# Scores, transposes and weighted sums of all attention heads two weight tiles later in a two-layer encoder trunk

## The chip, the cores and the metric

The kernel runs on one core of one Trainium2 chip. The time is device microseconds of one execution; the kernel before takes 844.85 us, the median of 3 runs (843.68 to 844.89). A core has five engines that work side by side: PE (matrix products), DVE, ACT and POOL (elementwise work) and SP, which here only issues transfers. Each works through its own instructions in the order in which they stand, and waits where one needs what another engine or a transfer has not delivered yet.

## The reference

A trunk of two layers on 256 frames of 1024 features. Each layer normalizes x, projects it with w_in, and gives the columns to four mixers: A, attention in chunks with a table of position biases; B, latent attention with a rotary key; C, attention with a forgetting gate; D, a causal convolution of 31 taps. Each of A, B and C has 4 heads of 64. Their outputs are projected, gated, summed and projected again; an MLP with squared ReLU follows.

```python
def hybrid_layer(x, positions, ...):
    h = rms_norm(x, g_mix)
    a_q, a_k, a_v, b_qlat, b_kvlat, b_krope, c_q, c_k, c_v, c_f, d_val, d_gate = split(h @ w_in)
    out_a = chunk_band_attention(a_q, a_k, a_v, rel_bias)          # 4 heads
    q = rms_norm(b_qlat, g_q_lat) @ w_uq                           # and rotary embedding of a part
    kv = rms_norm(b_kvlat, g_kv_lat) @ w_ukv
    out_b = block_causal_attention(q, k, v, CHUNK)                 # 4 heads; k: kv's and the rotary key
    log_f = log_sigmoid(c_f + b_forget)
    out_c = block_causal_attention(c_q, c_k, c_v, 1, cumsum(log_f))   # 4 heads
    out_d = silu(layer_norm(causal_conv(d_val * sigmoid(d_gate), w_dw) + b_dw))
    proj = einsum('bsnc,ncd->bsnd', [out_a, out_b, out_c, out_d], w_branch)
    gates = sigmoid(h @ w_gate + b_gate)
    x = x + sum(gates * proj, axis=2) @ w_o
    hf = rms_norm(x, g_ffn)
    return x + square(relu(hf @ w_up)) @ w_down
```

## The kernel before

**Weights.** All weights stream through the core once, as tiles of 128x1024 float32 (512 KB; a few are smaller). `weights` (line 102 on) makes one tile ready: SP issues its transfer into `raw` (line 110; five buffers), ACT rounds it to `hi` (line 114), and `lo` = raw − hi is made at line 115 on DVE, or, while `share[1]` is 2, on POOL for every second tile. Each product is then three matmuls that add up (`mm3`, lines 122 to 124): high by high, high by low and low by high. A tile of w_in, of the values or of the gates keeps PE busy for some 2.8 us.

**Stages of a layer.** `qk(0)` and `qk(2)` take two w_in tiles each (queries and keys of mixer A; then the convolution's input), `values` four tiles (v0 to v3 here; product pv), `mla` the tiles uq and ukv of mixer B, `qk(4)` and `qk(6)` two tiles each; then 32 tiles of gates, two per call of `gates(g)`, 8 tiles of the branches (`branch(m)`, product pbr), 8 of w_o (product po, into the four PSUM banks that held the halves of the last two branches' pbr, each free when line 737 has read it), and the MLP (w_up, w_dn).

**Small work between the tiles.** After each weight tile the code calls `tick()`, which runs the next entry of a list, `side`. Attention is spread over it: head i has its scores at entry A0 + 2i, its transposes three entries later and its weighted sum four entries later. Heads 0 to 3 are mixer A's, 4 to 7 B's, 8 to 11 C's. The other entries have fixed numbers: the latents of mixer B at 0 with their transposes at 1 to 3 (plt; their low half is latl, line 294), the rotary key's transposes (pkr, line 449) at 4, the rotary tables at 5, the forgetting sums at 13, the convolution's taps (cacc, lines 488 and 491) at 4 to 24, its normalization at 25 to 29.

```python
        NT = A0 + 2 * NH + 3
        plan = [[] for _ in range(NT)]
        for i in range(NH):
            plan[A0 + 2 * i].append((2, scores, i))
            plan[A0 + 2 * i + 3].append((1, transposes, i))
            plan[A0 + 2 * i + 4].append((0, weighted, i))
        ...
        for g in range(16):
            gates(g)
            if side:
                continue
            share[1] = 0
            if nbr < 0:
                conv_silu(last_exp[0])
            else:
                branch(nbr)
```

Entry 0 is run after qk(0)'s first tile, entry 4 after v0, entry 6 after v2, entry 8 after mla, entries 13 + 2g and 14 + 2g after the two tiles of `gates(g)`. When the list is empty, share[1] goes to 0, and each later call of `gates` is followed by one piece: first `conv_silu`, then one branch each. The branches that are left come one behind the other after the last gates.

**What `scores` does** (line 555 on): two matmuls into S from the queries and keys (qkA for mixer A; DVE writes it at lines 634 and 636); for a head of mixer A, SP issues the transfer of its bias table `bt` (192 KB, line 558, two buffers), and POOL writes two memsets into it (line 560) as soon as it is there. DVE and ACT follow with the softmax.

**What `branch` does**: eight products for each of two halves a into pbr; DVE multiplies each half by the gates Z (line 737, yt); POOL adds the parts (lines 738 and 739); ACT rounds the sum to yh (line 740); DVE makes the low half yl (line 741).

**What sets the order.** PE's instructions stand in the order of the code. Those of the other engines are put in order by a scheduler when the kernel is built, by its own estimate, so the diff alone doesn't tell it.

Of the kernel before, what the change touches and what calls it, by code (L numbers as in the profile page):

```python
# [44 lines left out]
NSMALL = 123  # L45


A0 = 4
CONV_FROM, CONV_TO = 4, 25
WARM = 9  # L50

# [19 lines left out]
def hybrid_trunk(ctx: ExitStack, tc: tile.TileContext, xT, xtok, pos, small, gfin, abias, w_lat, w_v, w_in, w_uq, w_ukv,  # L71
# [253 lines left out]
    for l in range(L):  # L325
# [349 lines left out]
        NH = 3 * HEADS  # L675
# [6 lines that stand above are left out]
        side = [[(lambda f=f, i=i: f(i)) for _, f, i in sorted(p, key=lambda e: e[0])] for p in plan]  # L682
# [285 lines left out]
```

## Time and profile before

| | us |
|---|---|
| median of 3 runs | 844.85 (843.68 to 844.89) |
| profiled execution | 845.43 |
| its span | 843.6 |
| outside the span | 1.8 |
| PE busy | 826.0 (98%) |
| DVE busy | 569.9 (68%) |
| ACT busy | 450.0 (53%) |
| POOL busy | 152.7 (18%) |

The span is the time from the first to the last instruction that the profiler recorded. The names L110, L115 and so on are lines of the kernel's code. PE at 98% means that all stretches in which PE stood still sum up to some 18 us, of which a part lies at the very start and the very end. The matmul records overlap (a matmul's start is 0.23 us or 0.12 us behind the one before it, while its own duration is longer), so on PE one reads the starts. "Idle before" in brackets is the time for which an engine had nothing to do ahead of an instruction, with the instruction whose end released it.

### The profile page before, as it was taken

Reading aid. Unit: us, or ns where it says so; the run is one execution under the profiler, and the core shown is the slowest. Engines: PE = TensorE matmul, PEld = TensorE weight load, DVE = VectorE, ACT = ScalarE, POOL = GpSimd, SP = SyncE. Lnnn points to the kernel's source line nnn. Section 1 sums busy time; section 2 is a strip of 40 time slices with the busy share of each in tenths; the row PEclk is TensorE's granted clock in tenths of the full one; section 3 lists DMA queues with packets and bytes.
Section 4 is the critical chain, followed back from the end, with each engine's and each line's share of the span. In section 5 each row is a group of like instructions: output and inputs, shape, how many; then the busy total and the mean of one; then the engine's idle time right before and its main releaser. Section 6 shows DMA issues by size and latency. Waiting matters only on the chain.

```text
span 843.6 us, 14520 instructions
## 1 busy us (share of the span) xinstructions
PE 826.0 (98%) x5646; PEld 759.5 (90%) x5646; DVE 569.9 (68%) x950; ACT 450.0 (53%) x759; POOL 152.7 (18%) x156
## 2 busy tenths in 40 slices
PE   9989999999999999999999999999999999999996
PEld 8969999999889999999899899999998899999994
DVE  7889984787665555555578899557866655555554
ACT  6745646654464444544485764485445554545443
POOL 6524332124200000000004332312331000000000
PEclk9999999999999999999999999999999999999999
DMA  8655433555546555555554544345555555555531
GB/s 281 232 181 181 132 126 126 166 184 185 165 164 198 189 189 186 186 189 187 172 176 161 188 132 145 132 131 174 194 176 200 175 186 190 191 185 186 188 126 50
DMA packets 42549, 145.55 MB, mean 173 GB/s; under 512 B 5104, under 2 KB 7408, under 8 KB 42352
## 3 DMA queue, kind: packets, MB, share of 16 engines
q1 hardware_dynamic: 41904, 142.98, 52.1%
q10 hardware_dynamic: 576, 1.64, 0.5%
q8 instruction: 44, 0.72, 0.4%
q14 instruction: 25, 0.20, 0.1%
HBM read 143.55 MB, written 1.05 MB: 171 GB/s over the span
## 4 chain that ended last, share of the span: by engine, by line
PE 89%; DVE 5%; issue 2%; POOL 1%; ACT 1%; DMA 0%; SPq 0%; POOLq 0%; DVEq 0%; ACTq 0%
PE pgt L122 7%; PE pgt L123 7%; PE pgt L124 7%; PE pu L123 7%; PE pu L124 7%; PE pu L122 7%; PE pd L123 7%; PE pd L122 7%; PE pd L124 7%; PE S L555 2%; DVE lo L115 2%; PE pqk L122 2%; PE pPV L593 2%; PE pqk L123 2%; PE pqk L124 2%
## 5 line engine op out<-in xcount | busy, mean ns | idle before, releaser
L115 DVE TENSOR_TENSOR lo<-raw,hi 128x1024 fp32r<-128x1024 f32 (+3 forms) x241 | 300.5, 1250 | 195.9 <-ACT hi L114 193.9
L114 ACT CAST hi<-raw 128x1024 fp32r<-128x1024 f32 (+2 forms) x273 | 278.5, 1024 | 266.0 <-issue 208.0
L122 PE MATMUL pgt<-xgh,hi 128*128 128x256 f32 x512 | 149.5, 292 | 0.0
L122 PE MATMUL pu<-xgh,hi 128*128 128x256 f32 x512 | 144.9, 283 | 0.7 <-ACT xgh L293 0.7
L123 PE MATMUL pu<-xgl,hi 128*128 128x256 f32 x512 | 145.1, 283 | 0.3
L124 PE MATMUL pu<-xgh,lo 128*128 128x256 f32 x512 | 144.9, 283 | 0.0
L123 PE MATMUL pgt<-xgl,hi 128*128 128x256 f32 x512 | 144.7, 283 | 0.0
L124 PE MATMUL pgt<-xgh,lo 128*128 128x256 f32 x512 | 144.7, 283 | 0.0
L122 PE MATMUL pd<-hi,u 128*128 128x512 f32 x256 | 100.8, 394 | 1.6 <-ACT u L803 1.6
L123 PE MATMUL pd<-hi,u 128*128 128x512 f32 x256 | 100.7, 393 | 1.1 <-DVE u L804 1.1
L122 PEld LDWEIGHTS pu<-xgh,hi 128*128 128x128 f32 x512 | 98.0, 191 | 3.4 <-ACT xgh L293 1.1
L123 PEld LDWEIGHTS pu<-xgl,hi 128*128 128x128 f32 x512 | 98.0, 191 | 3.0 <-DVE xgl L294 0.7
L124 PE MATMUL pd<-lo,u 128*128 128x512 f32 x256 | 99.6, 389 | 0.0
L122 PEld LDWEIGHTS pgt<-xgh,hi 128*128 128x128 f32 x512 | 97.9, 191 | 0.8 <-issue 0.3
L123 PEld LDWEIGHTS pgt<-xgl,hi 128*128 128x128 f32 x512 | 98.1, 192 | 0.4
L124 PEld LDWEIGHTS pu<-xgh,lo 128*128 128x128 f32 x512 | 98.0, 191 | 0.0
L124 PEld LDWEIGHTS pgt<-xgh,lo 128*128 128x128 f32 x512 | 97.9, 191 | 0.0
L115 POOL TENSOR_TENSOR lo<-raw,hi 128x1024 fp32r<-128x1024 f32 (+1 forms) x32 | 77.4, 2419 | 111.2 <-ACT hi L114 106.5
L491 DVE SCALAR_TENSOR_TENSOR cacc<-up,sm,cacc 128x256 f32<-128x256 f32 x120 | 77.9, 693 | 0.0
L122 PEld LDWEIGHTS pd<-hi,u 128*128 128x128 f32 x256 | 48.3, 189 | 10.8 <-ACT u L803 2.4
L124 PEld LDWEIGHTS pd<-lo,u 128*128 128x128 f32 x256 | 48.1, 188 | 10.4
L123 PEld LDWEIGHTS pd<-hi,u 128*128 128x128 f32 x256 | 48.3, 189 | 9.7 <-DVE u L804 2.0
(255 smaller groups left out, 1358.3 us busy)
## 6 DMA issues: line engine op xcount, KB each, us to landing
raw<-in_w_gate SPq DMA_DIRECT2D x64, 512.0 KB, 3.7
raw<-in_w_up SPq DMA_DIRECT2D x64, 512.0 KB, 4.2
raw<-in_w_dn SPq DMA_DIRECT2D x64, 512.0 KB, 4.2
raw<-in_w_in SPq DMA_DIRECT2D x23, 512.0 KB, 4.2
raw<-in_w_br SPq DMA_DIRECT2D x16, 512.0 KB, 3.7
raw<-in_w_o SPq DMA_DIRECT2D x16, 512.0 KB, 4.3
raw<-in_w_v SPq DMA_DIRECT2D x8, 512.0 KB, 4.2
raw<-in_w_lat SPq DMA_DIRECT2D x8, 210.0 KB, 4.6
```

Of the source, the lines that this page charges most:

```text
L114: cut = nc.scalar.copy(hi[:, c:c + w], raw[:, c:c + w])
L115: done = eng.tensor_tensor(lo[:, c:c + w], raw[:, c:c + w], hi[:, c:c + w], op=ALU.subtract)
L122: nc.tensor.matmul(ps, sh, mh, start=first, stop=False)
L123: nc.tensor.matmul(ps, *((sl, mh) if late_mov else (sh, ml)), start=False, stop=False)
L124: nc.tensor.matmul(ps, *((sh, ml) if late_mov else (sl, mh)), start=False, stop=last)
L491: ins = nc.vector.scalar_tensor_tensor(cacc[:, c, :], up[:, c, j:j + T], wcol, cacc[:, c, :], op0=ALU.mult, op1=ALU.add)
L555: nc.tensor.matmul(sl, q[:, b * P:(b + 1) * P], k[:, 0:n], start=True, stop=True)
L593: nc.tensor.matmul(po[o:o + 64, 0:T], v[:, 0, vo:vo + HD], pts[:, 0:T], start=True, stop=False)
```

## The change

One number: the entry of the list at which the first head's scores stand goes from 4 to 6.

```diff
--- before.py
+++ after.py
@@ -45,7 +45,7 @@
 NSMALL = 123
 
 
-A0 = 4
+A0 = 6
 CONV_FROM, CONV_TO = 4, 25
 WARM = 9
 
```

Scores, transposes and weighted sums of every head move two entries back, in both layers. The list has 33 entries instead of 31, so it is empty after g = 9 instead of g = 8: one more lo per layer is made by POOL, and conv_silu and the branches between the gates begin one call of `gates` later, so that three branches instead of two follow the last gates. All fixed entries stay.

On PE, behind the first values tile (v0, pv; numbers behind a name count the kernel's tiles), this stood before:

```order
L122 MATMUL pv_680<-hi_682,xgh_164 128x512
L123 MATMUL pv_680<-hi_682,xgl_165 128x512
L124 MATMUL pv_680<-lo_683,xgh_164 128x512
L555 MATMUL S_699<-qkA_381 128x128 [waits DVE_49]
L555 MATMUL S_699<-qkA_381 128x256
L449 MATMUL pkr_717<-ident,kr_70_585 128x128 [waits PE_49]
L449 MATMUL pkr_717<-ident,kr_70_585 128x128
L122 MATMUL pv_679<-hi_727,xgh_164 128x512 [waits Activation_49]
```

And now:

```order
L122 MATMUL pv_680<-hi_682,xgh_164 128x512
L123 MATMUL pv_680<-hi_682,xgl_165 128x512
L124 MATMUL pv_680<-lo_683,xgh_164 128x512
L449 MATMUL pkr_699<-ident,kr_70_585 128x128 [waits DVE_49]
L449 MATMUL pkr_699<-ident,kr_70_585 128x128
L122 MATMUL pv_679<-hi_709,xgh_164 128x512 [waits Activation_49]
L123 MATMUL pv_679<-hi_709,xgl_165 128x512
L124 MATMUL pv_679<-lo_710,xgh_164 128x512 [waits Pool_49]
```

S of the first head is gone from here (it stands behind the third values tile, v2), and pkr, which stays, is now the first to wait for DVE.

On SP, from the transfer behind v0 on, before (in_w_v are the values tiles v1 to v3, in_abias the tables bt):

```order
L558 DMA bt_702<-in_abias 128x384
L110 DMA raw_726<-in_w_v 128x1024
L110 DMA raw_753<-in_w_v 128x1024
L558 DMA bt_774<-in_abias 128x384
L110 DMA raw_792<-in_w_v 128x1024
L110 DMA raw_821<-in_w_uq 128x1024
```

And now:

```order
L110 DMA raw_708<-in_w_v 128x1024
L110 DMA raw_735<-in_w_v 128x1024
L558 DMA bt_756<-in_abias 128x384
L110 DMA raw_774<-in_w_v 128x1024
L558 DMA bt_860<-in_abias 128x384
L110 DMA raw_797<-in_w_uq 128x1024
```

Both tables moved: the first behind v2, the second behind v3. On POOL the tables' memsets stand where they stood; after the change it reads (lo_644 is the low half of the fourth w_in tile, lo_710 that of v1, lo_776 that of v3; before, the rows are the same but for the tables' numbers, and the values' lo's carry 728 and 794):

```order
L115 TENSOR_TENSOR lo_543<-raw_541,hi_542 128x1024
L231 MEMSET tq 128x2x64 x2
L560 MEMSET bt_756 64x64 x2
L560 MEMSET bt_860 64x64 x2
L115 TENSOR_TENSOR lo_644<-raw_642,hi_643 128x1024
L115 TENSOR_TENSOR lo_710<-raw_708,hi_709 128x1024
L115 TENSOR_TENSOR lo_776<-raw_774,hi_775 128x1024
```

The memsets of both tables stay ahead of lo_644.

On DVE, around the last two branches of layer 0 (yt_2629 is branch 6, yt_2672 branch 7, each with two halves; lo_2749 and lo_2767 are low halves of w_o tiles), before:

```order
L737 TENSOR_TENSOR yt_2629<-pbr_2630,Z_1099 128x512
L737 TENSOR_TENSOR yt_2629<-pbr_2644,Z_1099 128x512
L115 TENSOR_TENSOR lo_2749<-raw_2747,hi_2748 128x1024
L741 TENSOR_TENSOR yl_1992<-yt_2629,yh_1991 128x256
L737 TENSOR_TENSOR yt_2672<-pbr_2673,Z_1099 128x512
L737 TENSOR_TENSOR yt_2672<-pbr_2687,Z_1099 128x512
L115 TENSOR_TENSOR lo_2767<-raw_2765,hi_2766 128x1024
```

And now, where branch 5 (yt_2586) belongs to the group:

```order
L737 TENSOR_TENSOR yt_2586<-pbr_2587,Z_1076 128x512
L737 TENSOR_TENSOR yt_2586<-pbr_2601,Z_1076 128x512
L115 TENSOR_TENSOR lo_2731<-raw_2729,hi_2730 128x1024
L741 TENSOR_TENSOR yl_2054<-yt_2586,yh_2053 128x256
L737 TENSOR_TENSOR yt_2629<-pbr_2630,Z_1076 128x512
L737 TENSOR_TENSOR yt_2629<-pbr_2644,Z_1076 128x512
L115 TENSOR_TENSOR lo_2749<-raw_2747,hi_2748 128x1024
L737 TENSOR_TENSOR yt_2672<-pbr_2673,Z_1076 128x512
L741 TENSOR_TENSOR yl_2054<-yt_2629,yh_2053 128x256
L737 TENSOR_TENSOR yt_2672<-pbr_2687,Z_1076 128x512
```

Branch 5's yt and yl now stand directly ahead of branch 6's, and yl of branch 6 between the two halves of branch 7's yt.

## Rows read from the trace of the kernel before

**Rows 1.** The page: busy time of the engines, and the chain by engine.
```profile
PE 826.0 (98%) x5646; PEld 759.5 (90%) x5646; DVE 569.9 (68%) x950; ACT 450.0 (53%) x759; POOL 152.7 (18%) x156
...
PE 89%; DVE 5%; issue 2%; POOL 1%; ACT 1%; DMA 0%; SPq 0%; POOLq 0%; DVEq 0%; ACTq 0%
```
**Rows 2.** Waits of PE, whole span: us in total, times, longest us.
```profile
PE S L555 <- DVE qkA L636: 3.3, 1, 3.3
...
PE po L122 <- DVE yt L737: 0.6, 2, 0.3
```
**Rows 3.** Timeline of PE, 46.1 to 51.6: start us, us, instruction, idle before.
```profile
46.23 0.39 PE L124 MATMUL pv<-lo,xgh 128*128 128x512 f32 x1
49.91 0.92 PE L555 MATMUL S<-qkA 64*128 64x128 f32 x4 [3.29 <-DVE qkA L636]
```
**Rows 4.** Stretch by engine: us, busy (instructions) PE to POOL, PEclk, DMA, GB/s.
```profile
51.30:54.60 3.30, 3.30 (x9) 2.63 (x8) 3.30 (x11) 3.23 (x8) 0.00 (x0) 0.50 0.56 204
```
**Rows 5.** Timeline of DVE, 38 to 51.
```profile
38.20 3.35 DVE L115 TENSOR_TENSOR lo<-raw,hi 128x1024 fp32r<-128x1024 f32 x1
...
44.20 3.39 DVE L491 SCALAR_TENSOR_TENSOR cacc<-up,sm,cacc 128x256 f32<-128x256 f32 x3
47.52 1.21 DVE L115 TENSOR_TENSOR lo<-raw,hi 128x1024 fp32r<-128x1024 f32 x1
48.65 0.47 DVE L294 SCALAR_TENSOR_TENSOR latl<-plt,sm,lath 128x256 fp32r<-128x256 f32 x1
...
49.44 0.74 DVE L636 TENSOR_TENSOR qkA<-pqk,rb 128x256 f32<-128x256 f32 x2
```
**Rows 6.** Timeline of POOL, 29 to 48.
```profile
37.86 0.23 POOL L560 MEMSET bt<- 64x64 f32 x2 [4.53 <-DMA bt<-in_abias]
38.06 5.75 POOL L115 TENSOR_TENSOR lo<-raw,hi 128x1024 fp32r<-128x1024 f32 x2
```
**Rows 7.** Timeline of SP, 28 to 42: start of each issue.
```profile
28.80 0.33 SPq L110 DMA_DIRECT2D raw<-in_w_v  x1
29.18 0.42 SPq L558 DMA_DIRECT2D bt<-in_abias  x1
...
32.72 0.43 SPq L558 DMA_DIRECT2D bt<-in_abias  x1
35.51 0.33 SPq L110 DMA_DIRECT2D raw<-in_w_v  x1
40.49 0.33 SPq L110 DMA_DIRECT2D raw<-in_w_uq  x1
```
**Rows 8.** DMA issues of Rows 7's first four: KB each, us from issue to landing.
```profile
raw<-in_w_v SPq DMA_DIRECT2D x1, 512.0 KB, 3.8
...
bt<-in_abias SPq DMA_DIRECT2D x1, 192.0 KB, 3.9
...
bt<-in_abias SPq DMA_DIRECT2D x1, 192.0 KB, 5.1
...
raw<-in_w_v SPq DMA_DIRECT2D x1, 512.0 KB, 6.9
```
**Rows 9.** Timeline of PE, 40.3 to 41.1.
```profile
40.87 0.28 PE L124 MATMUL pqk<-xgh,lo 128*128 128x256 f32 x1
```
**Rows 10.** Timeline of DVE, 212 to 223, last branches of layer 0.
```profile
215.06 1.28 DVE L737 TENSOR_TENSOR yt<-pbr,Z 128x512 f32<-128x512 f32 x2
...
219.91 0.43 DVE L741 TENSOR_TENSOR yl<-yt,yh 128x256 fp32r<-128x256 f32 x1 [2.45 <-ACT yh L740]
220.26 1.28 DVE L737 TENSOR_TENSOR yt<-pbr,Z 128x512 f32<-128x512 f32 x2
```
**Rows 11.** Timeline of PE, 217.7 to 222.5, first products of w_o.
```profile
217.86 0.40 PE L122 MATMUL po<-hi,yh 128*128 128x512 f32 x1
...
221.09 0.47 PE L122 MATMUL po<-hi,yh 128*128 128x512 f32 x1 [0.31 <-DVE yt L737]
```
**Rows 12.** Timeline of DVE, 624 to 634, last branches of layer 1.
```profile
630.51 0.43 DVE L741 TENSOR_TENSOR yl<-yt,yh 128x256 fp32r<-128x256 f32 x1 [2.44 <-ACT yh L740]
```

## The prediction

> **What bounds the kernel now.** I read the page first: PE is busy for 826.0 us of the span and the chain of work that ended last is 89% PE, 5% DVE [rows 1]. So nearly every us of the kernel is matmul time, which this change doesn't touch (the number of matmuls stays), and what can move are the stretches in which PE stands still. The list of PE's waits gives them: the largest is one wait of 3.3 us of the first score product S for DVE's qkA of line 636; among the rest are 0.6 us in two places of po for DVE's yt of line 737 [rows 2]. Then I read PE's own timeline at the first of them: the first values tile's last matmul starts at 46.23, S at 49.91, "3.29" idle [rows 3]. So PE is free at 46.62 and gets going at 49.91. Behind it PE's granted clock is 0.50 for 3.3 us, from 51.3 to 54.6 [rows 4], its lower level of 1.2 GHz: work of 3.3 us there would be 1.65 us at full clock, so the wait costs 3.29 + 1.65, about 4.9 us in all. This is the most that taking the wait away could bring.
>
> DVE's timeline says why qkA is late. In order it does a lo (subtraction that makes the low half of a weight tile) in 3.35 us at 38.20, where the same shape takes 1.21 at 47.52; three convolution taps (cacc) in 3.39; the lo of 47.52; and latl at 48.65 [rows 5]. In the same stretch POOL runs two lo's, 38.06 to 43.81 [rows 6]. So DVE is slow there because POOL works beside it.
>
> **The change, part by part.** A0 from 4 to 6 moves scores, transposes and weighted sums of all 12 heads two weight tiles back, in both layers, and whatever hangs on the last of them by one gates pair (two tiles).
>
> (1) The first heads. PE's next instruction behind the first values tile is no longer S but pkr (transpose of the rotary key), which isn't moved. In the order of after, pkr waits for a DVE instruction too: latl, which shares its PSUM pool of two buffers. In the trace of before that latl is the one that starts at 48.65 and takes 0.47 [rows 5], so it ends at 49.12. If nothing else moved, PE would wait from 46.62 to 49.17: 2.55 instead of 3.29, a gain of 0.74 and no more. The wait would change its name, not go.
>
> (2) But S brings its bias table along. Each of the first four heads has SP load bt (192 KB) and POOL write two memsets into it, and both are issued where the scores stand. Before, SP's order is v0, bt0, v1, v2, bt1, v3 (v: values tiles); in the order of after it is v0, v1, v2, bt0, v3, bt1. POOL's order is the same in both at this place: memsets of bt0, memsets of bt1, then the lo of the fourth w_in tile (lo_644). So that lo now stands behind a table which is loaded behind the fourth values tile. Its dates: SP issues v3 at 35.51 [rows 7] and it lands after 6.9 us [rows 8], at 42.4. bt lands some 0.5 us after the tile ahead of it: v0 28.80 + 3.8 = 32.6, bt0 29.18 + 3.9 = 33.1 [rows 7, 8]. As v3 now has one table fewer ahead of it (0.5 us) and bt1 comes behind it, bt1 lands between 42.4 and 42.9; I take 42.75. (Before: 32.72 + 5.1 = 37.8 [rows 7, 8], and POOL's memsets start at 37.86 at once, after an idle 4.53 [rows 6].) From landing to the start of the lo it was 38.06 − 37.82 = 0.24. The first of the two lo's takes 38.06 to 40.49, the moment at which SP issues the uq tile that waits for it [rows 6, 7]: 2.43. So lo_644 is ready at 42.75 + 0.24 + 2.43 = 45.42. PE needs it at the first L124 of that tile, 40.87 [rows 9]; before, it was there 0.4 us ahead. **PE waits 4.55 us** at a place where it didn't wait.
>
> Bounds of this: landing 42.4 and 2.43 for the lo give 4.2; landing 42.9 and 3.3 for the lo (the second of the two lo's, 5.75 − 2.43 [rows 6]) give 5.6. I take 2.43, since what lengthened the second was DVE's lo of 38.20, which is over by then.
>
> The Trainium skill ("SBUF — State Buffer", section "Who interferes with whom") says that a DVE instruction with two SBUF inputs and a GpSimd one that reads SBUF shut each other out for the whole instruction, whichever starts first. The trace agrees: 38.06 + 2.43 = 40.49 is when DVE's blocked lo could start, and with 1.06 more it ends at 41.55, as its row says; POOL's second lo then ran from there to 43.81. By that rule the moved lo would lose at most one tap of DVE, about 0.5 us, and the upper end would be 5.2 instead of 5.6; the sum stays.
>
> What the stall takes over: the first values tile then ends at 46.62 + 4.55 = 51.17. DVE has meanwhile worked on without POOL beside it (its lo of 38.20 in 1.21), and even in before's slow order latl is done at 49.12, qkA of line 636 at 49.44 + 0.74 without the stall. So pkr at 51.17 doesn't wait, and S, two tiles on, doesn't either. Net of (1) and (2): −3.29 + 4.55 = **+1.26 us**.
>
> (3) The clock. Before, a stop of 3.29 us was followed by 3.3 us at 0.50 [rows 3, 4]. A stop of 4.55 will be followed by such a stretch too; I take the same cost, 1.65, and so a difference of 0. From no such stretch to twice the one of before it is −1.65 to +1.65.
>
> (4) Layer 1's start. There the tables of heads 0 and 1 are loaded during layer 0 and PE doesn't wait at S at all (the wait list has it once [rows 2]). Nothing to gain; 0.
>
> (5) The end of attention. The plan is over one gates pair later. Before, 7 of the 8 branch products stand between gates pairs, and branches 6 and 7 back to back at the end; after, 6, so branches 5, 6 and 7 follow each other and then w_o. A branch takes PE 2.86 us, but its sum goes DVE yt (two products of 0.64), POOL two additions, ACT yh, DVE yl, and yl is in DVE's queue ahead of the next branch's yt: yt of branch 6 starts at 215.06, yl at 219.91 after an idle 2.45, yt of branch 7 at 220.26 [rows 10]. So one turn of it takes 5.2 us against PE's 2.86. In before, PE comes out of branch 7 at 217.86, has four PSUM banks to reuse in w_o, and waits for the third, freed by yt of branch 7: due 217.86 + 12 × 0.23 = 220.62, started 221.09 [rows 11], 0.47 late. After, with T the end of branch 5 on PE: yt(5) T + 0.06; yl(5) 4.85 later at T + 4.9; yt(6) T + 5.26 to 6.46; a lo; the first half of yt(7) T + 7.6 to 8.25; yl(6) T + 5.26 + 4.85 = 10.1; the second half of yt(7) T + 10.45 to 11.1, as the order puts it behind yl(6). PE ends branch 7 at T + 5.72. First bank: free with half of yt(6), T + 6.09 in place of 5.72, 0.37. Third bank, T + 8.85: free since 8.25. Fourth, due at T + 10.23: free at 11.3, 1.07. Together 1.44 against 0.47: **+0.97 in each layer** (layer 1 has the same shape, yl at 630.51 after 2.44 idle [rows 12]), +1.94. Bounds: 0.25 a layer, if only the first bank is late by more than before, and 1.5, if the fourth is late by another half turn.
>
> (6) One more lo per layer on POOL, since share[1] stays 2 for one pair longer. POOL is busy for 18% of the span [rows 1] and takes 2.4 us for it instead of DVE's 1.21. Cover: POOL's idle time; where it stands ahead of POOL's small power of the convolution's variance, up to 1 us a layer could show. I take 0.
>
> Sum: +1.26 + 0 + 1.94 = **+3.2 us**. The profiled execution, 845.43 us with a span of 843.6, would become 848.6; it is 0.58 above the median of the runs, so the median of 844.85 becomes **848.0**.
>
> **Rivals.**
> A. *The wait goes as the change says* (faster). bt1 lands early enough for lo_644, and DVE has latl done by 46.6: −3.29 − 1.65 + 1.94 = −3.0, 841.8. For it: the table has only 192 KB, and DVE needs just 2.6 us less work. Against it: SP's order puts the table behind v3, and in before DVE worked without a break up to 49.1 while POOL ran its lo's early.
> B. *The table is in time, latl isn't* (same). Wait of 2.55 at pkr instead of 3.29, clock as before, tails: −0.74 + 1.94 = +1.2, 846.0. It decides if bt1 lands before 38.2, as its 192 KB would if transfers in flight at once shared evenly. For a landing in between, say 40, the lo ends at 42.7, PE waits 1.8, and the sum lies between A and B, near 844, same too.
> C. *The tails don't show* (same): only +1.26, 846.1. It decides if the scheduler's order of yl and yt costs PE nothing, as where POOL and ACT are faster than in [rows 10].
> D. *A second stretch at 0.50* (slower): the stop of 4.55 costs twice 1.65, or POOL's extra lo shows with 1 us: +5 to +6, 850.0.
>
> **How the numbers follow.** The measurement can tell about 0.2%, 1.7 us, from no change: faster is below 843.2, slower above 846.5. Forecast 0.58, A 0.09, B 0.15, C 0.10, D 0.08. Slower: forecast and D, 0.66; same: B and C, 0.25; faster: A, 0.09. The forecast's own bounds are +1.26 −0.35 to +1.05 and tails 0.5 to 3.0: 846.3 to 850. To hold 8 in 10 the range takes in B and C below and most of D: 845.6 to 850.2; A and the lowest of B lie outside.
>
> **What would show it.** Step 2: a wait of PE of 4 to 5 us at L124 of pqk for POOL's lo at about 40.9, POOL's memset idle until 42.4 or later, and no wait at S. If instead the list names pkr with 2.5 us, B holds; if it names neither, A. Step 3: a stretch at 0.50 right behind the stall. Step 5: waits of po for yt of 1 to 1.5 us in each layer in place of 0.6 in all; if these are gone, C. The forecast is wrong as a whole if bt's transfer overtakes the tile ahead of it.

## The result

The changed kernel takes 857.03 us, the median of 4 runs (856.68 to 857.37), against 844.87 for the kernel before: the ratio is 1.0146, with a 95% interval of 1.0129 to 1.0164. It is slower by 12.2 us; the forecast was 3.2 us slower, 848.0 with a range of 845.6 to 850.2. The sign was right, the size was not.

The page of the kernel after, its span and its busy times:

```profile
span 855.1 us, 14522 instructions
...
PE 826.5 (97%) x5646; PEld 759.5 (89%) x5646; DVE 579.3 (68%) x948; ACT 449.2 (53%) x759; POOL 156.2 (18%) x158
```

PE is busy as long as in [rows 1] (826.5 against 826.0), so the 11.5 us by which the span grew from 843.6 are time in which PE stands still. The list of PE's waits, to be held against [rows 2] (us in total, times, longest):

```profile
PE pPV L593 <- ACT pts L584: 6.4, 8, 1.3
PE pqk L124 <- POOL lo L115: 5.6, 1, 5.6
...
PE po L122 <- DVE yt L737: 1.5, 2, 0.8
...
PE plat L122 <- ACT hi L114: 1.0, 2, 0.5
```

The wait of 3.3 us at S is gone. In its place stands the stall at L124 of the fourth w_in tile that the prediction worked out, 5.6 us; the waits of w_o grew by 0.9 us; and eight waits of pPV (the weighted sums of the heads, line 593) for ACT's pts (the copy of the transposed probabilities, line 584), 6.4 us, are new. The prediction has no step for these. The plat waits lie ahead of 20 us, where the two kernels have the same order: PE's first 22 us simply ran 0.4 us later in this execution.

**The stall.** POOL between 29 and 56, SP between 28 and 60, and the two transfers with their us to landing, in the kernel after:

```profile
38.54 0.23 POOL L560 MEMSET bt<- 64x64 f32 x2 [5.54 <-DMA bt<-in_abias]
44.41 0.23 POOL L560 MEMSET bt<- 64x64 f32 x2 [5.64 <-DMA bt<-in_abias]
44.61 4.66 POOL L115 TENSOR_TENSOR lo<-raw,hi 128x1024 fp32r<-128x1024 f32 x2
```

```profile
35.91 0.33 SPq L110 DMA_DIRECT2D raw<-in_w_v  x1
36.28 0.86 SPq L558 DMA_DIRECT2D bt<-in_abias  x1
```

```profile
raw<-in_w_v SPq DMA_DIRECT2D x1, 512.0 KB, 8.0
...
bt<-in_abias SPq DMA_DIRECT2D x1, 192.0 KB, 8.1
```

The second table landed at 36.28 + 8.1 = 44.4, POOL's lo started at 44.61, and PE went on at 46.99:

```profile
46.99 0.58 PE L124 MATMUL pqk<-xgh,lo 128*128 128x256 f32 x1 [5.56 <-POOL lo L115]
```

The clock behind it, from the busy times by stretch (the third number from the right is the granted clock):

```profile
46.30:46.90 0.60, 0.00 (x0) 0.00 (x0) 0.00 (x0) 0.00 (x0) 0.60 (x1) 0.62 0.00 0
46.90:49.80 2.90, 2.81 (x13) 2.81 (x14) 0.00 (x0) 0.00 (x0) 2.37 (x2) 0.50 0.61 204
49.80:53.00 3.20, 3.20 (x21) 2.90 (x21) 1.59 (x5) 1.42 (x2) 0.77 (x1) 0.99 0.95 331
```

PE worked 2.9 us at its lower level, 1.45 us lost, against 1.65 in [rows 4]. This holds for this one execution; in the traces of four experiments with the same stall the stretch at 0.50 is twice as long (last section).

**The waits of pPV.** The first stands at 84.61, "1.22" idle. DVE, then ACT, then POOL and PE of the kernel after, around it:

```profile
75.72 1.21 DVE L115 TENSOR_TENSOR lo<-raw,hi 128x1024 fp32r<-128x1024 f32 x1
76.85 3.40 DVE L491 SCALAR_TENSOR_TENSOR cacc<-up,sm,cacc 128x256 f32<-128x256 f32 x3
80.17 1.72 DVE L634 SCALAR_TENSOR_TENSOR QC<-pqk,rb 64x256 f32<-64x256 f32 x4
81.92 0.29 DVE L570 CUSTOM_DVE_ANT_0 neg<-S,bt 128x128 f32<-128x128 f32 x1
```

```profile
82.26 0.40 ACT L572 ACTIVATE pe<-neg,mn 128x128 f32<-128x128 f32 x1 [5.77 <-DVE mn L570]
...
83.15 1.03 ACT L114 CAST hi<-raw 128x1024 fp32r<-128x1024 f32 x1
84.09 0.47 ACT L584 COPY pts<-pT 128x384 f32<-128x384 f32 x1
```

```profile
76.57 2.61 POOL L115 TENSOR_TENSOR lo<-raw,hi 128x1024 fp32r<-128x1024 f32 x1 [0.92 <-ACT hi L114]
```

```profile
76.20 0.92 PE L555 MATMUL S<-qkA 64*128 64x128 f32 x4
...
84.61 0.65 PE L593 MATMUL pPV<-pts,VAC 128*64 128x256 f32 x2 [1.22 <-ACT pts L584]
```

PE finishes S of a head (the third of mixer A) at about 77.1. DVE's first step of its softmax (neg, line 570) comes only at 81.92, since three convolution taps, 3.40 us beside POOL's lo of 76.57, and four copies stand ahead of it in DVE's queue. ACT's exp (pe) waits for it for 5.77 us; and behind pe, in ACT's queue, stands pts, which belongs to the head before and whose own input has been there since 80.5. PE is through with the tile ahead at 83.4 and waits 1.22 us for pts. So one late DVE instruction holds, through ACT's order, a matmul of another head. In the kernel before, the same entry of the list holds the scores of the fourth head (S at 75.79), and DVE does this there:

```profile
73.77 1.21 DVE L115 TENSOR_TENSOR lo<-raw,hi 128x1024 fp32r<-128x1024 f32 x1
74.91 1.27 DVE L491 SCALAR_TENSOR_TENSOR cacc<-up,sm,cacc 128x256 f32<-128x256 f32 x3
76.10 0.85 DVE L634 SCALAR_TENSOR_TENSOR QC<-pqk,rb 64x256 f32<-64x256 f32 x2
76.98 0.29 DVE L570 CUSTOM_DVE_ANT_0 neg<-S,bt 128x128 f32<-128x128 f32 x1
```

There the taps are through when POOL's lo starts (at 76.16), and neg comes 1.2 us behind the start of S instead of 5.7. The kernel after also puts four of the copies ahead of neg instead of two. Over all 24 heads neg starts 1.0 to 3.4 us behind S in the kernel before, and no pPV waits; in the kernel after seven heads of each layer are 2.2 to 5.7 us behind, and four of each layer's weighted sums wait.

### The profile page after: what moved, and what is told of

It is laid out like the page before. It is cut to its first block, busy times and chain, and to the rows that moved or that the text cites. A ratio compares the mean times of both kernels' runs of the same rounds, so it can differ in the third digit from the quotient of the medians.

```text
span 855.1 us, 14522 instructions
## 1 busy us (share of the span) xinstructions
PE 826.5 (97%) x5646; PEld 759.5 (89%) x5646; DVE 579.3 (68%) x948; ACT 449.2 (53%) x759; POOL 156.2 (18%) x158
## 4 chain that ended last, share of the span: by engine, by line
PE 88%; DVE 3%; ACT 3%; issue 2%; POOL 2%; DMA 1%; SPq 0%; POOLq 0%; DVEq 0%; ACTq 0%
PE pgt L122 7%; PE pu L123 7%; PE pgt L123 7%; PE pu L124 7%; PE pu L122 7%; PE pgt L124 7%; PE pd L123 7%; PE pd L122 7%; PE pd L124 7%; PE S L555 2%; ACT hi L114 2%; PE pPV L593 2%; PE pqk L122 2%; PE pqk L124 2%; PE pqk L123 1%
## 5 line engine op out<-in xcount | busy, mean ns | idle before, releaser
L115 DVE TENSOR_TENSOR lo<-raw,hi 128x1024 fp32r<-128x1024 f32 (+3 forms) x239 | 296.9, 1245 | 190.1 <-ACT hi L114 189.7
L124 PE MATMUL pu<-xgh,lo 128*128 128x256 f32 x512 | 144.9, 283 | 0.0
L124 PE MATMUL pgt<-xgh,lo 128*128 128x256 f32 x512 | 144.6, 283 | 0.0
L115 POOL TENSOR_TENSOR lo<-raw,hi 128x1024 fp32r<-128x1024 f32 (+1 forms) x34 | 81.1, 2385 | 118.3 <-ACT hi L114 113.7
L124 PE MATMUL pd<-lo,u 128*128 128x512 f32 x256 | 99.6, 389 | 0.0
L124 PEld LDWEIGHTS pu<-xgh,lo 128*128 128x128 f32 x512 | 98.0, 191 | 0.0
L124 PEld LDWEIGHTS pgt<-xgh,lo 128*128 128x128 f32 x512 | 97.9, 191 | 0.0
L491 DVE SCALAR_TENSOR_TENSOR cacc<-up,sm,cacc 128x256 f32<-128x256 f32 x120 | 92.1, 809 | 0.0
L124 PEld LDWEIGHTS pd<-lo,u 128*128 128x128 f32 x256 | 48.1, 188 | 10.4
```

The lines of the kernel that those rows point to most:

```text
L115: done = eng.tensor_tensor(lo[:, c:c + w], raw[:, c:c + w], hi[:, c:c + w], op=ALU.subtract)
L124: nc.tensor.matmul(ps, *((sh, ml) if late_mov else (sl, mh)), start=False, stop=last)
L491: ins = nc.vector.scalar_tensor_tensor(cacc[:, c, :], up[:, c, j:j + T], wcol, cacc[:, c, :], op0=ALU.mult, op1=ALU.add)
```

## The experiments

All are compared with runs of the kernel before on the same chip (medians of 845.6, 845.2 and 845.1 in the three groups). "Less than the kernel after" is the difference of two medians out of different groups of runs.

**Tables early.** Undoes one part: the tables are loaded at the entries of before.

```diff
+            if i < HEADS:
+                plan[4 + 2 * i].append((3, table, i))    # the transfer and the two memsets of bt
             plan[A0 + 2 * i].append((2, scores, i))
```

> The kernel after, but the bias tables of heads 0 to 3 are loaded (and get their memsets) at the list entries at which they stood in the kernel before (4, 6, 8, 10), while scores, transposes and weighted sums stay two entries later. Theory: PE's wait of 5.6 us at L124 of the fourth w_in tile comes from the table that is loaded behind the fourth values tile and holds POOL's queue. Then this wait is gone. What takes its place is PE's wait for pkr: at most 2.5 us (latl at 49.1 as in the kernel before), with or without a stretch at clock 0.50; if DVE is in time, none. Time 850 without a wait at pkr, 852.5 with 2.5 us, 854 with the low clock too. Rival: the wait has another cause (POOL slow by itself, lo late in any order): wait and time stay, 857. The eight waits of pPV (6.4 us in all) stay under either.

852.16 us, ratio 1.0081 (1.006 to 1.0102), 4.9 less than the kernel after. PE's waits there:

```profile
PE pPV L598 <- ACT pts L589: 6.5, 8, 1.3
PE pkr L449 <- DVE latl L294: 2.4, 1, 2.4
```

The stall is gone, and what the prediction called the wait under a new name is there: 2.4 us at pkr, where 2.55 was worked out. Behind it the clock stays at 1.00:

```profile
49.30:52.60 3.30, 3.30 (x17) 2.77 (x18) 3.30 (x10) 1.76 (x5) 0.00 (x0) 1.00 0.85 290
```

PE, DVE, ACT and POOL have the order of the kernel after here, and only SP's differs. So the stall is shown to come from the tables' place in SP's order. By these two executions it cost its 5.6 less 2.4, and the 1.45 of its slow stretch: 4.6, of 4.9 measured.

**Softmax first.** Orders taps behind neg.

```diff
+                last_neg[0] = nc.vector.tensor_tensor_reduce(out=neg...
                 after(ins, share[2])                     # ins: one tap
+                if last_neg[0] is not None:
+                    after(ins, last_neg[0])
```

> The kernel after, but each convolution tap on DVE is ordered behind the first softmax step (neg, from S) of the last head whose scores stand ahead of it in the code. Theory T1: PE's eight waits of pPV for ACT's pts come from DVE's order: neg stands behind taps and gate or query copies, so exp is late on ACT, and pts is queued behind exp. Then all eight are gone, 6.4 us by the list plus some 0.2 us each for matmuls that restart: 849 to 850.5. Rival T2: the taps are merely slow beside POOL's lo, and whichever stands first the sum of DVE's work is late: the waits stay or move to DVE's lo, 855 to 857. The wait at L124 stays at 5.6 under either.

850.06 us, ratio 1.0056 (1.0034 to 1.0078), 7.0 less than the kernel after. No wait of pPV is left. DVE at the place shown above, now:

```profile
76.91 1.72 DVE L637 SCALAR_TENSOR_TENSOR QC<-pqk,rb 64x256 f32<-64x256 f32 x4
78.66 0.29 DVE L573 CUSTOM_DVE_ANT_0 neg<-S,bt 128x128 f32<-128x128 f32 x1
```

neg starts 1.6 us behind S (77.02) instead of 5.7. So moving the taps out of the way is enough. But the taps got shorter by it, too: all 120 that run at this line are busy for 72.8 us here, for 92.1 in the kernel after and for 77.9 in the kernel before. Whether their place alone made the waits is the next question.

**Short lo on POOL.**

```diff
+            if eng is nc.gpsimd and share[0] > 13:
+                done = eng.tensor_tensor(lo[:, 0:128], raw[:, 0:128], hi[:, 0:128], op=ALU.subtract)
+                eng.memset(lo[:, 128:n].bitcast(F32), 0.0)
```

> The kernel after, but from the second values tile on POOL subtracts only the first 128 of a tile's 1024 columns and writes zeros into the others (this leaves out most of the low halves of these tiles). The order of the instructions on PE, DVE and ACT is that of the kernel after. Theory T2: the eight waits of pPV need POOL's long lo beside DVE's taps (three taps took 3.4 us beside it, 1.3 alone), which makes DVE late: then they are gone, 849 to 850.5, with taps at 0.4 us each. Rival T1: DVE's order alone, neg behind taps, is enough: the waits stay above 4 us in all, 854 to 857.

849.62 us, ratio 1.0055 (1.0033 to 1.0077), 7.4 less than the kernel after, and no wait of pPV, with the taps still ahead of neg in DVE's order. DVE there, and POOL:

```profile
64.79 0.46 DVE L495 SCALAR_TENSOR_TENSOR cacc<-up,sm,cacc 128x256 f32<-128x256 f32 x1
...
75.05 1.27 DVE L495 SCALAR_TENSOR_TENSOR cacc<-up,sm,cacc 128x256 f32<-128x256 f32 x3
76.24 1.72 DVE L638 SCALAR_TENSOR_TENSOR QC<-pqk,rb 64x256 f32<-64x256 f32 x4
77.99 0.29 DVE L574 CUSTOM_DVE_ANT_0 neg<-S,bt 128x128 f32<-128x128 f32 x1
```

```profile
64.76 0.84 POOL L117 MEMSET lo<- 128x896 f32 x1 [6.10 <-PE pv L128]
...
76.18 0.85 POOL L117 MEMSET lo<- 128x896 f32 x1 [1.92 <-PE pqk L128]
77.15 0.45 POOL L116 TENSOR_TENSOR lo<-raw,hi 128x128 fp32r<-128x128 f32 x1
```

So T1 alone falls: the order is harmless where POOL doesn't slow the taps. By the two runs the waits need both, taps ahead of neg and POOL's long lo beside them, with the reservation that the other order had shortened the taps as well. The Trainium skill ("SBUF — State Buffer", section "Who interferes with whom") has the reason: a DVE instruction with two SBUF inputs, as a tap is, and a GpSimd one that reads SBUF exclude each other, and a GpSimd memset, which only writes, does not disturb it. The traces agree: the tap at 64.79 runs within the memset of 64.76 and takes 0.46, and the three taps of this place take 1.27 here and 3.40 beside the long lo. In the kernels before and after, each tap that took over 0.5 us (15 and 21 of 120) overlaps a lo of POOL.

**Taps later.**

```diff
-CONV_FROM, CONV_TO = 4, 25
+CONV_FROM, CONV_TO = 6, 27
```

> The kernel after, but the convolution's taps too are two entries later (6 to 26 instead of 4 to 24, and its normalization with them), so that taps and heads stand to each other as in the kernel before. Theory T3: the pPV waits come from where the heads stand against the taps: then they are gone, 849 to 850.5. Rival T4: they come from DVE being late from the start of the attention on, whichever entries the taps have: they stay, 856 to 858.

858.26 us, ratio 1.0158 (1.0133 to 1.0183); ten waits of pPV, 7.3 us. T3 falls: it is not the distance of taps and heads in the list that matters. T4 stands as far as this goes. What is left is where heads and taps stand against the weight tiles, and so against POOL's lo's and the copies; no run tries that by itself.

**Layer 1 only.**

```diff
+        A0 = 6 if l == 1 else 4
```

> Heads two entries later in layer 1 alone; layer 0 as in the kernel before. Theory: the move costs layer 1 its share of the pPV waits (3.2 us by the list, 3.5 with restarts) and 0.4 at the tail, and nothing at the start: 848.5 to 849.5. Rival: the lateness of DVE in both layers starts from the stall at the start of layer 0 and its shift of the timeline, so that layer 1 alone costs only the tail: 845 to 846.

849.16 us, ratio 1.005 (1.0032 to 1.0068), 4.05 us over before. The list has the old wait of S and half of the new ones:

```profile
PE pPV L592 <- ACT pts L583: 3.2, 4, 1.3
PE S L554 <- DVE qkA L635: 3.1, 1, 3.1
```

The pPV waits don't need the stall of layer 0: each layer makes its own four.

**Branches early.** Undoes another part.

```diff
-            if side:
+            if len(side) > 2:
                 continue
```

> The kernel after, but conv_silu and the branches begin when two entries of the list are left, so that after as before seven branches stand between the gates and two follow each other at the end, and POOL makes one lo less per layer. Theory: three branches in a row cost the 1.5 us of waits of po for yt, against 0.6 before: 0.9 us less by the list, 856. If the tail is worth what was predicted (1.9 us) 855. Rival: nothing hangs on it, 857.0.

856.36 us, ratio 1.013 (1.0111 to 1.0148), 0.7 less than the kernel after. The waits of po fall from 1.5 to 1.0 us, and not to the 0.6 of before. The intervals don't tell 0.7 from none, and in this execution the stall at L124 was 0.6 us shorter as well (5.0), so the 0.5 us of the wait list is all that is seen of the tails here.

**X later.**

```diff
-            after(nc.scalar.dma_start(X, xtok), dsig)
+            after(nc.scalar.dma_start(X, xtok), w[3])    # w: the tile uq, in mla
```

> The kernel after, but the transfer of X (1 MB, on ACT's queue), which runs beside that of the fourth values tile, is issued only at the tile uq. In the order of this kernel POOL's fourth w_in lo then stands ahead of the tables' memsets. Theory: the table itself lands earlier without X beside it (in the kernel after it landed 8.1 us after its issue), by up to 3 us; and since POOL's lo doesn't stand behind it, PE's wait of 5.6 us at L124 is gone, a wait at pkr of up to 2.5 us takes its place: 851 to 853, as with the early tables. Rival: the lo is late for its own reasons and PE waits at L124 as before: 857. The waits of pPV stay under either.

852.43 us, ratio 1.0082 (1.0053 to 1.0111). The stall is gone, and 2.3 us at pkr stand in its place; seven waits of pPV, 5.1 us, stay. The last two transfers of the values:

```profile
raw<-in_w_v SPq DMA_DIRECT2D x1, 512.0 KB, 6.0
...
bt<-in_abias SPq DMA_DIRECT2D x1, 192.0 KB, 6.1
```

More than one thing changed, though, DVE's order of qkA and latl too: the table lands 2 us sooner without X beside it, but it would still have been late (41.9); that PE doesn't wait is due to POOL's order, in which the lo now stands ahead of the memsets.

**All three, and the rotary key later.**

> The kernel after with all three edits: tables early, softmax step ahead of the taps, branches one call earlier. If the three causes are separate and are all there is, only the start differs from the kernel before: 840 if pkr doesn't wait (its 3.3 us of wait and 1.65 us of low clock are gone), 844 with a wait of 2.5 us at pkr and the low clock. Rival: a fourth cause remains, over 846.

842.24 us, ratio 0.9968 (0.9954 to 0.9981). The single edits took 4.9, 7.0 and 0.7 off the kernel after, 12.6 in all, and together 14.8 (by the spans of the profiled executions 11.6 and 12.9). By the ratios, each to the runs of the kernel before in its own group, they are worth 5.5, 7.6 and 1.4, 14.5 in all, against 15.0 together, so that the three add up within the intervals. What is left against the kernel before is the start: 2.4 us at pkr at clock 1.00 instead of 3.3 at S with a slow stretch.

```diff
-        side[4].append(rotary_key_rows)
+        side[6].append(rotary_key_rows)
-            side[5].append(rotary_tables)
+            side[7].append(rotary_tables)
```

> The kernel with all three edits (tables early, softmax step ahead of the taps, branches one call earlier), and besides the rotary key's transposes (pkr) two entries later, behind S of the first head, and the rotary tables (pcs) two entries later. In the kernel with three edits PE still waits 2.4 us at pkr for DVE's latl. Theory: behind the first values tile nothing then waits for DVE any more, and 2.4 us go: 839.8. Rival: the wait moves on to S or pcs, which need DVE's work of the same time: 841 to 842.5.

841.03 us, ratio 0.9954 (0.9937 to 0.9971). PE doesn't wait at all between the first values tile and the end of attention. Only half of the 2.4 us shows in the medians, 3.0 in the spans; the runs don't settle which.

**Softmax first without the move.** The control of the second experiment, on the kernel before.

> The kernel before (scores from entry 4), with the taps ordered behind the softmax's first step as in the second experiment. There are no waits of pPV in the kernel before. Theory: the 7 us that this order took off the kernel after were brought in by the move, and the order is worth nothing without it: 844 to 846. Rival: it is a gain in any case (DVE's and ACT's later work comes sooner): 838 to 842.

841.01 us, ratio 0.9959 (0.9943 to 0.9975). The rival holds, and this is the most useful run of all. PE doesn't wait at S; 0.7 us at L124 for POOL's lo are new in its list. DVE, around the first head:

```profile
45.67 0.47 DVE L294 SCALAR_TENSOR_TENSOR latl<-plt,sm,lath 128x256 fp32r<-128x256 f32 x1
46.06 0.74 DVE L639 TENSOR_TENSOR qkA<-pqk,rb 128x256 f32<-128x256 f32 x2
...
49.23 0.29 DVE L573 CUSTOM_DVE_ANT_0 neg<-S,bt 128x128 f32<-128x128 f32 x1 [1.84 <-PE S L558]
```

No tap runs ahead of neg, so qkA is made at 46.06 instead of 49.44 [rows 5], and S starts when PE gets there. One edit that leaves the heads where they were gives as much as the move with four repairs. So the old wait can be taken away with the heads where they are: what made it were the taps ahead of qkA in DVE's queue.

## Why the prediction was wrong

**(1) and (2), the start: right in mechanism, a little small.** The wait changes its name, the table behind the fourth values tile holds POOL's lo, PE stalls at L124: all as worked out, and the tables' experiment gives 2.4 at pkr against 2.55. The stall was 5.56 instead of 4.55, still inside the bounds of 4.2 to 5.6; over the runs with this order it is 4.8 to 5.7. The term that was small is the landing of v3: 8.0 us where I took the 6.9 of [rows 8] and even less. Net +2.27 instead of +1.26. One reading was incomplete: the prediction puts DVE's slowness in the kernel before down to POOL's two lo's, 38.06 to 43.81, but the three taps of 44.20 that took 3.39 [rows 5] ran beside a third:

```profile
44.75 2.57 POOL L115 TENSOR_TENSOR lo<-raw,hi 128x1024 fp32r<-128x1024 f32 x1 [0.94 <-ACT hi L114]
```

So the effect that decided the case, taps that meet POOL's lo, was in the rows; it was priced for the moved lo and for nothing behind it.

**(3), the clock: right in the profiled execution.** 1.45 us lost against 1.65; the term of 0 was off by 0.2. In the traces of four experiments with the same stall PE worked 4.7 to 5.5 us at 0.50, 2.4 to 2.7 lost, which is inside the bounds; that the term came out so near is partly luck.

**(4), layer 1's start: right**; no wait there.

**(5), the tails: right in place, almost twice too large.** po waits 0.77 and 0.75 us, once per layer, in place of twice 0.31: +0.9 by the list, and +1.1 by the starts of the matmuls, as the prediction counts, instead of +1.94. At the first bank PE is 0.1 us late, where 0.37 was predicted; the fourth is late, as the order of yl between the two halves of yt said.

**(6), the extra lo on POOL: nothing of it is seen.** Right.

**The step that failed is one that isn't there.** The sum goes from the start of attention straight to its end. Between lie some 25 weight tiles per layer in which every head's softmax runs through DVE and ACT, and the prediction left them at zero without naming what hides them. They cost 6.4 us by the list and 7.0 by the experiment, more than all other terms together. What hid them was the slack of the chain from S over neg and exp to pts: a neg 3.4 us behind its S (115.2 and 118.6) still cost nothing in the kernel before; at the place shown above it came 1.2 us behind S, and in the kernel after 5.7. A late neg then keeps itself late: ACT's next hi and pts stand behind exp, DVE's next lo behind that hi, the taps behind that lo, and the next neg behind the taps. The first late neg of layer 0 is that of the second head, 2.2 us behind its S against 1.1 in the kernel before, and ahead of it a tap at 66.13 takes 2.36 us beside POOL's lo. Shown by experiment, with the reservation made there, is that both the taps ahead of neg and POOL's long lo are needed; that the loop keeps up the lateness is read from the trace and was not tried by itself.

The second experiment's span is 6.7 us below that of the kernel after, but its trace has the longer stretch at 0.50. Layer 1 has no such stretch in these traces: by the starts of the same PE instructions it is 4.3 us longer in the kernel after than in the kernel before, and 0.6 longer with the softmax first, so that the waits cost 3.7 a layer, 7.4 in both. With 0.4 at the head, 2.3 − 0.2 at the start and 1.1 in the tails this makes 11.0 of the 11.5 us of span; 0.5 are not assigned.

**The rivals.** A, the wait simply goes, did not come from the move; it came from the taps' order. B's mechanism, the wait at pkr, is what the kernel with early tables shows. C did not happen, since the tails show. Of D, the extra lo shows nothing; the longer slow stretch is not in the profiled execution of the kernel after, but is in those of four experiments with the same stall. None of the four held the pPV waits.

## What to carry to other kernels

When work is moved along a list, cost the whole stretch that it is moved through and not only its two ends: ask for each engine in between how far it runs ahead of the one that waits for it, since a lead of a few us is soon used up: here three small instructions took 2.1 us longer because they met another engine's work. Before moving the waiting work, look at what stands ahead of its producer in that engine's queue: ordering filler behind it took the same wait away without touching the rest. And whatever a moved step issues on other queues, a transfer and a memset here, moves with it and can hold a queue that has nothing to do with it.

## What the runs showed of the hardware

PE's clock after a stop: the same stop did not have the same price. Behind stops of 2.4 us (tables early, and all three edits) the clock stayed at 1.00; behind 2.3 us (X later) it was 0.50 for some 3.3 us, and once more in that run, 1.9 us after a wait of pPV of 1.2 us. Behind 3.29 us (before) it was 0.50 for 3.3 us, behind 3.1 us (layer 1 only) for 6.7. Behind 5.56 us (after) it had fallen 0.5 us before PE went on, and 2.9 us of work ran at 0.50; with the same stall, of 4.8 to 5.7 us, in softmax first, short lo, taps later and branches early the stretch lasted some 6.7 us. First softmax first, then X later:

```profile
45.20:51.90 6.70, 5.18 (x25) 5.18 (x25) 0.07 (x1) 0.24 (x1) 3.79 (x2) 0.50 0.62 206
```

```profile
48.90:52.20 3.30, 3.30 (x9) 2.72 (x10) 3.30 (x10) 1.47 (x4) 0.00 (x0) 0.50 0.83 284
83.10:86.30 3.20, 3.20 (x17) 3.20 (x17) 3.15 (x7) 0.00 (x0) 1.50 (x1) 0.50 0.46 154
```

The 35 runs of the kernel before in the three groups show what this does to a time: with a mean granted clock of 0.997 or 0.998 they take 842.6 to 843.5 us, with 0.995 or 0.996 844.0 to 846.0, with 0.994 846.3 to 847.2. So a difference of one or two us between two medians, as that of branches early, can be the clock alone.

With a transfer of 1 MB on ACT's queue in flight, two transfers on SP's queue took 2 us longer to land (8.0 and 8.1 us in the kernel after against 6.0 and 6.1 in X later), and the table still landed 0.5 us behind the tile ahead of it in both.
